# Two-layer hybrid block on one core: the FFN's middle down-projection sums are added to y by DMA after a ScalarE copy, not by VectorE

## The chip, the cores and the metric

The kernel runs on one core of a Trainium2 chip. The metric is the device time of one execution in microseconds (us), taken on the chip; a profile of one execution is kept beside the timed runs. Engines are named as the profile names them: PE is TensorE (matmuls), PEld its weight loads, DVE is VectorE, ACT is ScalarE, POOL is GpSimd and SP is SyncE, which here only issues DMAs. Each engine works through its own list of instructions in a fixed order and waits on semaphores where it needs another engine's result.

## The reference, cut to what matters

Two layers act on x (512 tokens, 1024 channels) and, in the first layer only, on ctx (256 tokens). Each layer has a mixing half (attention, a Fourier mix, a long convolution) and a feed-forward half (the FFN). Only the FFN is touched:

```python
def conv_ffn(h, w_up, w_c, b_c, w_down):
    u = dwconv3(h @ w_up, w_c, b_c)
    gate, val = jnp.split(u, 2, axis=-1)
    return (jax.nn.silu(gate) * val) @ w_down

fx = rmsnorm(x, g_pre_ffn[i]) * (1.0 + sc2) + sh2
yx = conv_ffn(fx, w_up[i], w_ffn_conv[i], b_ffn_conv[i], w_down[i])
x = x + ga2 * rmsnorm(yx, g_post_ffn[i])
```

All numbers are float32, D_FF is 2816, that is 22 blocks of 128 channels. In layer 0 the same is done for ctx.

## The kernel before, in words

**Products.** Float32 products are made of three passes: a matrix is split into a rounded high part and the low rest (`split`, lines 181 and 182: ACT writes the high part, DVE, or POOL where it is given, subtracts to get the low part), and `mm3` (lines 196 to 198) issues high·high, high·low and low·high.

**FFN of x, `ffn_x`.** For each block m of 128 hidden channels, two weight tiles `r` of w_up are loaded by SP, combined by POOL into `tt` (lines 1276 to 1279; the up product is done in a Strassen-like form of seven block products), split by ACT and DVE into `Wh` and `Wl`, and multiplied into four narrow PSUM tiles `pn` (pool of 4 tiles, 128x512) with the activations, which are the streams `h`. ACT and DVE gather the results into `C` (lines 1298 to 1326), ACT and DVE do the depthwise convolution (`ft`, lines 636 to 638), ACT the silu (line 1334), POOL the product of gate and value (line 1335), and ACT and DVE split it into `gT`.

**The down product, `ffn_down`.** It works on groups of blocks: two at a time (in `ffn_x` the last group has four). For a group it loads and splits the rows of w_down (`Wr` to `Wh`, `Wl`), and for each tile t of 128 tokens (4 for x, 2 for ctx) it sums the group's products into a wide PSUM tile `pw` of 128x1024. That pool holds two tiles, so the third t can only begin when the first has been read out. The sums over the groups are gathered in SBUF in `y`, one tile of 128x1024 for each t:

- the first group is copied to `y` by ACT (line 1200),
- each middle group is added to `y` by one DVE instruction (line 1202),
- the last group is added in halves by DVE (line 1196), and goes on to the norm and the residual.

For ctx there are 9 middle groups with 2 tiles, for x 8 with 4 tiles in each of two layers: 18 + 32 + 32 = 82 additions on line 1202.

**FFN of ctx, `ffn_c`,** runs in layer 0 ahead of `ffn_x`, with plain up products (tiles `L` of w_up, product in `pn`, lines 1228 and 1229 for silu and product, `gc` for the split result). There the low parts of w_down are made by POOL. The matmuls that make the modulation (tiles `wm` of w_mod, line 283) run between them.

**Order.** The generators yield estimates of their cost and lag, and `Net.go`, `pump` and `step` interleave them in program order. The tile framework then schedules each engine's list with its own timing model, and adds the waits on semaphores; so the order of the instructions can change when a single one is exchanged. SBUF tiles of 128x1024 come from a pool `M` with 27 buffers, which also holds `y`, `gT`, the streams `h`, the gains `G` and the pieces `w` of w_up. A tile from a pool waits until the last reader of that buffer is done.

Of the kernel before, what the change touches and what calls it, by code (L numbers as in the profile page):

```python
# [8 lines left out]
F32 = mybir.dt.float32  # L9
# [3 lines left out]
ALU = mybir.AluOpType  # L13
# [55 lines left out]
class Net:  # L69
# [1095 lines left out]
    def ffn_down(self, l, st, g, ms, begin, el=None, early=0, mid=None):  # L1165

        nc = self.nc
        end = ms[-1] == MF - 1
        if begin and st is self.X:
            st.y = [self.M("y", F32) for _ in range(st.NT)]  # L1170
        wd = {k: self.load_w(self.I["w_down"][l, k], el=nc.gpsimd if el else None) for k in ms}
        if end:
            ss = [self.small("ss", 2, 6) for _ in range(st.NT)]
            xr = [self.load_r(self.src[st.name][t]) for t in range(st.NT)]
        acc = {}

        def add(t, h, ks):
            hs, ts = slice(h * 512, (h + 1) * 512), slice(t * P, (t + 1) * P)
            if (t, h) not in acc:
                if h == 0:  # L1180
                    acc[t] = self.pw()
                acc[t, h] = acc[t][:, hs]
            for k in ks:
                self.mm3(acc[t, h], (g[k][:, 0, ts], g[k][:, 1, ts]), (wd[k][0][:, hs], wd[k][1][:, hs]), k == ms[0], k == ms[-1])
            yield 3 * len(ks) * C512, 0.0

        for t in range(early):
            for h in range(2):
                yield from add(t, h, ms[:-1])
        for t in range(st.NT):  # L1190
            y = st.y[t]
            for h in range(2):
                hs = slice(h * 512, (h + 1) * 512)
                yield from add(t, h, ms[-1:] if t < early else ms)
                if end:
                    nc.vector.tensor_tensor(y[:, hs], y[:, hs], acc[t, h], op=ALU.add)
                    self.sumsq_half(ss[t], y[:, hs], h)
                    nc.gpsimd.tensor_tensor(y[:, hs], y[:, hs], st.G[1][:, hs], op=ALU.mult)
            if begin:
                nc.scalar.copy(y, acc[t])  # L1200
            elif not end:
                nc.vector.tensor_tensor(y, y, acc[t], op=ALU.add)  # L1202
            else:
                self.tail(st, t, xr[t], ss[t])
                if t == Z["MT"] and mid:
                    yield from mid
# [495 lines left out]
```

## Time and profile before

| | us |
|---|---|
| median of 3 timed runs | 1789.37 |
| lowest and highest of these | 1785.97 and 1790.05 |
| the profiled execution | 1784.91 |
| its span in the trace | 1783.1 |
| its mean granted TensorE clock (share of full) | 0.971 |

Times in the trace are microseconds from the span's start. `ffn_c` fills the stretch from about 480 to 705, `ffn_x` of layer 0 the stretch from there to about 1080, and `ffn_x` of layer 1 that from about 1400 to the end. A group row of the profile names line, engine, operation and tiles, then the count, the busy time and the mean of one, and then how long the engine stood idle just before those instructions and which instruction ended the idle time. A busy PE is not a PE at its peak: the records of matmuls overlap, and the pace of a run of matmuls is read from the distance of their starts.

### The profile page before, as it was taken

Reading aid. Unit: us, or ns where it says so; the run is one execution under the profiler, and the core shown is the slowest. Engines: PE = TensorE matmul, PEld = TensorE weight load, DVE = VectorE, ACT = ScalarE, POOL = GpSimd, SP = SyncE. Lnnn points to the kernel's source line nnn. Section 1 sums busy time; section 2 is a strip of 40 time slices with the busy share of each in tenths; the row PEclk is TensorE's granted clock in tenths of the full one; section 3 lists DMA queues with packets and bytes.
Section 4 is the critical chain, followed back from the end, with each engine's and each line's share of the span. In section 5 each row is a group of like instructions: output and inputs, shape, how many; then the busy total and the mean of one; then the engine's idle time right before and its main releaser. Section 6 shows DMA issues by size and latency. Waiting matters only on the chain. (4 is left out here: it accounts for less than half of the span.)

```text
span 1783.1 us, 27842 instructions
## 1 busy us (share of the span) xinstructions
PE 1639.1 (92%) x10502; PEld 1397.4 (78%) x10502; DVE 1440.1 (81%) x2324; ACT 934.9 (52%) x1737; POOL 692.3 (39%) x515
## 2 busy tenths in 40 slices
PE   5799987899999997989999998998898799999997
PEld 2677775687788897878989885787787678889996
DVE  5888777697665688889988987668895878999997
ACT  2642344487565454556554556434773465555454
POOL 3343332000134337665554645212002455655543
PEclk9899999999999998999999999999999899999999
DMA  9214277603477642332342258653012343332323
GB/s 366 101 61 146 86 243 263 232 13 130 162 253 232 228 155 71 96 118 84 101 148 84 89 185 305 213 175 118 1 48 83 130 146 103 95 107 86 127 62 119
DMA packets 70003, 248.01 MB, mean 139 GB/s; under 512 B 8111, under 2 KB 9647, under 8 KB 69868
## 3 DMA queue, kind: packets, MB, share of 16 engines
q1 hardware_dynamic: 60716, 215.54, 35.6%
q0 software_dynamic: 9152, 30.68, 5.5%
q8 instruction: 83, 1.36, 0.3%
q14 instruction: 52, 0.43, 0.1%
HBM read 232.03 MB, written 14.16 MB: 138 GB/s over the span
## 5 line engine op out<-in xcount | busy, mean ns | idle before, releaser
L196 PE MATMUL pn<-h,Wh 128*128 128x256 f32 x1328 | 376.6, 286 | 11.7 <-DVE ft L638 4.3
L198 PE MATMUL pn<-h,Wl 128*128 128x256 f32 x1328 | 372.8, 284 | 10.2 <-DVE Wl L182 10.2
L197 PE MATMUL pn<-h,Wh 128*128 128x256 f32 x1328 | 374.2, 283 | 1.7 <-POOL h L182 1.7
L196 PEld LDWEIGHTS pn<-h,Wh 128*128 128x128 f32 x1328 | 253.2, 191 | 24.5 <-issue 7.8
L198 PEld LDWEIGHTS pn<-h,Wl 128*128 128x128 f32 x1328 | 252.1, 191 | 15.3 <-DVE Wl L182 12.7
L197 PEld LDWEIGHTS pn<-h,Wh 128*128 128x128 f32 x1328 | 253.8, 191 | 6.2 <-POOL h L182 2.4
L181 ACT CAST Wh<-Wr 128x1024 fp32r<-128x1024 f32 x118 | 122.7, 1049 | 138.9 <-PE pw L198 46.4
L182 DVE TENSOR_TENSOR Wl<-Wr,Wh 128x1024 fp32r<-128x1024 f32 x89 | 129.7, 1465 | 53.7 <-ACT Wh L181 53.2
L1276 POOL TENSOR_TENSOR tt<-r,r 128x512 f32<-128x512 f32 x44 | 75.0, 1705 | 233.9 <-DMA r<-w_up 211.0
L196 PE MATMUL pw<-Wh,gT 128*128 128x512 f32 x352 | 137.5, 404 | 9.0 <-ACT gT L181 3.9
L197 PE MATMUL pw<-Wl,gT 128*128 128x512 f32 x352 | 138.5, 396 | 3.1 <-DVE Wl L182 3.1
L198 PE MATMUL pw<-Wh,gT 128*128 128x512 f32 x352 | 137.8, 396 | 1.8 <-DVE gT L182 1.8
L181 ACT CAST Wh<-tt 128x1024 fp32r<-128x1024 f32 x88 | 90.8, 1048 | 84.9 <-PE pn L197 42.4
L182 DVE TENSOR_TENSOR Wl<-tt,Wh 128x1024 fp32r<-128x1024 f32 x88 | 122.5, 1411 | 11.0 <-ACT Wh L181 8.0
L1335 POOL TENSOR_TENSOR ft<-ft,ft 128x512 f32<-128x512 f32 x44 | 70.8, 1609 | 132.4 <-DVE ft L638 94.2
L1202 DVE TENSOR_TENSOR y<-y,pw 128x1024 f32<-128x1024 f32 x82 | 99.2, 1213 | 20.1 <-PE pw L198 20.0
L182 POOL TENSOR_TENSOR h<-tf,h 128x256 fp32r<-128x256 f32 (+1 forms) x40 | 36.0, 921 | 187.8 <-ACT h L181 186.5
L182 POOL TENSOR_TENSOR Wl<-Wr,Wh 128x1024 fp32r<-128x1024 f32 x29 | 74.6, 2578 | 57.7 <-ACT Wh L181 56.5
L1278 POOL TENSOR_TENSOR tt<-r,tt 128x512 f32<-128x512 f32 x44 | 75.8, 1722 | 51.9 <-DVE Wl L182 51.9
L196 PE MATMUL pw<-h,Wh 128*128 128x256 f32 (+1 forms) x224 | 76.9, 343 | 13.9 <-DVE v L638 2.6
L283 PE MATMUL pn<-wm,cpad 128*32 128x256 f32 x768 | 67.6, 411 | 19.7 <-DMA wm<-w_mod 19.3
L636 ACT ACTIVATE ft<-C,vec 128x512 f32<-128x512 f32 x88 | 68.7, 811 | 32.1 <-DVE C L1325 25.7
(361 smaller groups left out, 4706.1 us busy)
## 6 DMA issues: line engine op xcount, KB each, us to landing
wm<-w_mod SPq DMA_DIRECT2D x96, 512.0 KB, 5.4
r<-w_up SPq DMA_DIRECT2D x90, 512.0 KB, 3.6
Wr<-w_down SPq DMA_DIRECT2D x66, 512.0 KB, 3.8
L<-w_up SPq DMA_DIRECT2D x44, 512.0 KB, 4.4
Wr<-w_out SPq DMA_DIRECT2D x24, 512.0 KB, 3.6
Wr<-w_in_t SPq DMA_DIRECT2D x16, 512.0 KB, 3.9
dft<-hdft_x POOLq DMA_DIRECT2D x16, 512.0 KB, 4.1
Wr<-w_in_c SPq DMA_DIRECT2D x12, 512.0 KB, 3.6
```

The costliest lines, as they stand in the source:

```text
L181: r = nc.scalar.copy(hi, src)
L182: (el or nc.vector).tensor_tensor(lo, src, f32(hi), op=ALU.subtract)
L196: nc.tensor.matmul(ps, l[0], r[0], start=first, stop=False, **kw)
L197: nc.tensor.matmul(ps, l[0], r[1], start=False, stop=False, **kw)
L198: nc.tensor.matmul(ps, l[1], r[0], start=False, stop=last, **kw)
L283: nc.tensor.matmul(ps[32 * g : 32 * g + 32, cs], self.cpad[:, q % 2 * 4 + g, :], w[:, g, :], start=q % 2 == 0, stop=q % 2 == 1, skip_group ...
L636: nc.scalar.activation(dst, ps, AF.Identity, scale=w1, bias=b)
L1202: nc.vector.tensor_tensor(y, y, acc[t], op=ALU.add)
L1276: te.tensor_tensor(half(t13, 0), half(r[1], 0), half(r[0], 0), op=ALU.subtract)
L1278: te.tensor_tensor(half(t24, 0), half(r[1], 1), half(t13, 0), op=ALU.subtract)
L1335: nc.gpsimd.tensor_tensor(o[0], o[0], o[1], op=ALU.mult)
```

## The change

In the middle groups the sum in PSUM is now copied by ACT into a new tile `ya` of pool `M`, and POOL issues a DMA that adds `ya` to `y` in SBUF. The first and the last group are as before. Lines behind it are moved by three: 1276 is 1279 now, 1334 is 1337, 1335 is 1338.

```diff
             if begin:
                 nc.scalar.copy(y, acc[t])
             elif not end:
-                nc.vector.tensor_tensor(y, y, acc[t], op=ALU.add)
+
+                part = self.M("ya", F32)
+                nc.scalar.copy(part, acc[t])
+                nc.gpsimd.dma_start(y, part, accum_op=ALU.add)
             else:
                 self.tail(st, t, xr[t], ss[t])
```

So 82 instructions leave DVE, 82 copies (line 1204) come to ACT, and 82 DMA issues (line 1205) come to POOL. Outside the FFN the order of the instructions is nearly the same as before. What follows shows the fifth middle group of x in layer 1, on three engines.

VectorE before, where the four additions of a group stand between the splits of weights, the convolution and the gathering into `C`:

```order
L182 TENSOR_TENSOR gT_16437<-ft_16429,gT_16437 128x512
L1202 TENSOR_TENSOR y_14734<-y_14734,pw_16454 128x1024
L182 TENSOR_TENSOR w_16626<-r_16609,w_16626 128x512
L1202 TENSOR_TENSOR y_14735<-y_14735,pw_16468 128x1024
L1323 TENSOR_TENSOR C_16539<-C_16539,pn_16554 128x256
L1202 TENSOR_TENSOR y_14736<-y_14736,pw_16482 128x1024
L1325 TENSOR_TENSOR C_16510<-pn_16511,C_16510 128x256
L1326 TENSOR_TENSOR C_16539<-pn_16511,C_16539 128x256
L182 TENSOR_TENSOR Wl_16625<-tt_16617,Wh_16624 128x1024
L637 SCALAR_TENSOR_TENSOR ft_16633<-C_16510,vec_101,ft_16633 128x511
L1202 TENSOR_TENSOR y_14737<-y_14737,pw_16496 128x1024
```

On VectorE the change only takes these four rows out; the others stay in nearly this order. ScalarE at the same place before, from the split of `gT` on (`Wh` are high parts of weights, `ft` the convolution's input, `C` a gathered product):

```order
L181 CAST gT_16437<-ft_16429 128x512
L181 CAST w_16626<-r_16609 128x512
L181 CAST Wh_16624<-tt_16617 128x1024
L636 ACTIVATE ft_16633<-C_16510,vec_101 128x512
L636 ACTIVATE ft_16634<-C_16539,vec_101 128x512
L181 CAST Wh_16622<-tt_16616 128x1024
```

and ScalarE there now:

```order
L181 CAST gT_16569<-ft_16561 128x512
L1204 COPY ya_16599<-pw_16586 128x1024
L1204 COPY ya_16615<-pw_16602 128x1024
L181 CAST Wh_16764<-tt_16757 128x1024
L636 ACTIVATE ft_16773<-C_16650,vec_101 128x512
L636 ACTIVATE ft_16774<-C_16679,vec_101 128x512
L1204 COPY ya_16631<-pw_16618 128x1024
L1337 ACTIVATE ft_16773<-ft_16773 128x512
L181 CAST Wh_16762<-tt_16756 128x1024
L1204 COPY ya_16647<-pw_16634 128x1024
L181 CAST w_16766<-r_16749 128x512
```

Two copies stand together right behind the split of `gT`, which waits for POOL's product of gate and value; the third stands behind the convolution's two first passes, and the fourth three rows later. POOL before, two blocks of the same stretch:

```order
L1335 TENSOR_TENSOR ft_16429<-ft_16429,ft_16430 128x512
L1276 TENSOR_TENSOR tt_16752<-r_16745,r_16744 128x512
L1277 TENSOR_TENSOR tt_16752<-r_16745 128x512
L1278 TENSOR_TENSOR tt_16753<-r_16745,tt_16752 128x512
L1279 TENSOR_TENSOR tt_16753<-tt_16753,r_16744 128x512
L1335 TENSOR_TENSOR ft_16633<-ft_16633,ft_16634 128x512
```

and POOL there now:

```order
L1338 TENSOR_TENSOR ft_16561<-ft_16561,ft_16562 128x512
L1279 TENSOR_TENSOR tt_16892<-r_16885,r_16884 128x512
L1280 TENSOR_TENSOR tt_16892<-r_16885 128x512
L1205 DMA y_14834<-ya_16599 128x1024
L1205 DMA y_14835<-ya_16615 128x1024
L1281 TENSOR_TENSOR tt_16893<-r_16885,tt_16892 128x512
L1282 TENSOR_TENSOR tt_16893<-tt_16893,r_16884 128x512
L1205 DMA y_14836<-ya_16631 128x1024
L1338 TENSOR_TENSOR ft_16773<-ft_16773,ft_16774 128x512
```

On PE, the third sum of such a group began 17 narrow matmuls (128x256) behind the end of the second, and waited for DVE; now it begins 25 narrow matmuls behind it, waits for ACT, and the fourth follows at once. The first sum ends 8 wide matmuls (128x512) ahead of the second in both.

On POOL, the four DMA issues of a group (the fourth follows behind the last row) stand between the four subtractions that make `tt`, and each waits for its copy on ScalarE; the next product of gate and value stands behind three of them.

## The prediction

> **What bounds the kernel now.** I read the page's first part, then a table of the FFN's stretches, then in two of them the matmuls and what ended PE's waits. The page (span; busy time of each engine):
>
> ```profile
> span 1783.1 us, 27842 instructions
> PE 1639.1 (92%) x10502; PEld 1397.4 (78%) x10502; DVE 1440.1 (81%) x2324; ACT 934.9 (52%) x1737; POOL 692.3 (39%) x515
> ```
>
> PE and DVE are both heavily loaded; a share over the whole span doesn't say which holds the FFN. The stretches do (ctx FFN; its end and the start of `ffn_x`; layer 0's first blocks; layer 0's middle groups; layer 1's middle groups):
>
> ```profile
> core 0: us, PE busy (x) PEld busy (x) DVE busy (x) ACT busy (x) POOL busy (x), PEclk, DMA share, GB/s
> 480.00:660.00 180.00, 180.00 (x1324) 158.13 (x1323) 125.87 (x207) 99.69 (x158) 71.78 (x45) 1.00 0.67 226
> 660.00:705.00 45.00, 35.20 (x228) 31.99 (x227) 42.79 (x49) 20.55 (x35) 31.67 (x19) 0.89 0.25 76
> 705.00:790.00 85.00, 77.72 (x536) 72.21 (x536) 67.86 (x73) 49.61 (x80) 54.80 (x32) 0.96 0.32 103
> 790.00:1045.00 255.00, 245.22 (x1653) 223.97 (x1652) 233.41 (x287) 138.82 (x218) 134.29 (x79) 0.99 0.32 104
> 1490.00:1745.00 255.00, 251.49 (x1739) 232.20 (x1738) 237.39 (x261) 135.52 (x212) 128.62 (x77) 1.00 0.30 96
> ```
>
> In the ctx FFN PE never rests and DVE has 30% free. In the two stretches of x's middle groups DVE is busy 92% and 93%, PE 96% and 99%. How much PE could gain is read from its pace, since busy matmuls overlap. A run of narrow matmuls (128x256) and one of wide ones (128x512), first and last starts:
>
> ```profile
> 926.09 0.28 PE L196 MATMUL pn<-h,Wh 128*128 128x256 f32 x1
> ...
> 928.67 0.28 PE L197 MATMUL pn<-h,Wh 128*128 128x256 f32 x1
> ...
> 930.44 0.39 PE L197 MATMUL pw<-Wl,gT 128*128 128x512 f32 x1
> ...
> 935.34 0.39 PE L198 MATMUL pw<-Wh,gT 128*128 128x512 f32 x1
> ```
>
> 22 steps in 2.58 us are 0.117 us for a narrow matmul, 21 steps in 4.90 us are 0.233 us for a wide one. Now the matmuls of layer 0's middle groups, with the idle time before them and what ended it (each of the three passes has its group; those left out have the same count within two):
>
> ```profile
> L196 PE MATMUL pn<-h,Wh 128*128 128x256 f32 x355 | 100.2, 285 | 1.3 <-DVE C L1323 0.6 <-ACT C L1298 0.5 <-ACT C L1316 0.2
> L198 PE MATMUL pn<-h,Wl 128*128 128x256 f32 x354 | 98.4, 284 | 1.4 <-DVE Wl L182 1.4
> L197 PE MATMUL pw<-Wl,gT 128*128 128x512 f32 x126 | 49.7, 399 | 1.1 <-DVE Wl L182 1.1
> L198 PE MATMUL pw<-Wh,gT 128*128 128x512 f32 x126 | 49.4, 396 | 0.9 <-DVE gT L182 0.9
> L196 PE MATMUL pw<-Wh,gT 128*128 128x512 f32 x124 | 48.3, 404 | 5.0 <-ACT gT L181 2.8 <-ACT Wh L181 2.2
> L196 PE MATMUL pn<-h,w 128*128 128x256 f32 x60 | 17.1, 284 | 0.1
> ```
>
> 3x355 + 3x60 = 1245 narrow ones take 146 us at that pace, 376 wide ones 88, and some 32 small ones about 4: 238 of 255 us. So 17 us at most are to be had here; the waits listed are 9.8 of them, 4.0 ended by DVE (0.6+1.4+1.1+0.9) and 5.0 by ACT's `gT` and `Wh`. And layer 1:
>
> ```profile
> L196 PE MATMUL pn<-h,Wh 128*128 128x256 f32 x386 | 106.8, 281 | 1.1 <-DVE C L1323 1.1
> L198 PE MATMUL pw<-Wh,gT 128*128 128x512 f32 x129 | 50.8, 396 | 0.9 <-DVE gT L182 0.9
> L196 PE MATMUL pw<-Wh,gT 128*128 128x512 f32 x130 | 49.9, 399 | 1.5 <-ACT gT L181 0.8 <-DVE y L1202 0.7
> L198 PE MATMUL pn<-h,w 128*128 128x256 f32 x64 | 18.1, 282 | 0.0
> ```
>
> 3x386 + 3x64 = 1350 narrow ones are 158 us, 389 wide ones 91: 249 of 255, so 6 us at most, of which DVE ended 2.7 (1.1+0.9+0.7). **PE bounds the FFN, with DVE close behind it**: what the change can win is PE's few waits, not the DVE time that it frees.
>
> **The change part by part.** What leaves DVE, and what comes to ACT (group of the page; durations min/median/max of the first group's copies):
>
> ```profile
> L1202 DVE TENSOR_TENSOR y<-y,pw 128x1024 f32<-128x1024 f32 x82 | 99.2, 1213 | 20.1 <-PE pw L198 20.0
> ...
> L1200 ACT COPY y<-pw x10: 1002/1008/1017, 508.7 to 1470.7; 128x1024 f32<-128x1024 f32 x10
> ```
>
> DVE loses 82 x 1.213 = 99.2 us. In each of the two stretches that is 32 x 1.213 = 38.8 us: DVE falls from 233 to 195 and from 237 to 199 of 255, 78% at most, and no longer holds PE. ACT gains 82 x 1.008 = 82.7 us, 32.3 in each stretch: 139 to 171 and 136 to 168 of 255. That is hidden in ACT's idle time, as a load; as a place in a queue it isn't, which is the term of new waits below.
>
> Term 1, the hand-over at 700 us, where an addition itself holds PE:
>
> ```profile
> 697.44 4.17 DVE L182 TENSOR_TENSOR w<-r,w 128x512 fp32r<-128x512 f32 x2
> 701.53 2.34 DVE L1202 TENSOR_TENSOR y<-y,pw 128x1024 f32<-128x1024 f32 x2
> ...
> 702.80 0.58 PE L196 MATMUL pw<-h,Wh 128*128 128x256 f32 x1 [2.56 <-DVE y L1202]
> ...
> 705.76 0.37 ACT L1298 COPY C<-pw 128x256 f32<-128x256 f32 x1 [8.27 <-PE pw L198]
> ```
>
> PE waits 2.56 us for a sum to be read while DVE is behind and ACT stands idle for 8.27 us. A copy by ACT removes that wait: -2.6 us. Bounds: 0, and -4.9, since four additions (4 x 1.213) leave a DVE that is 95% busy there.
>
> Term 2, layer 0's middle groups: the 4.0 us ended by DVE go, and of the 5.0 ended by ACT I take half, since `gT` comes late through DVE's convolution but also through POOL: -6.5 us. Bounds: 0 and -17.
>
> Term 3, layer 1's: the 2.7 us ended by DVE go. Bounds: 0 and -6.
>
> Term 4, new waits. Two copies stand behind ACT's split of `gT`, which waits for POOL (total, times, longest, in layer 0's middle groups):
>
> ```profile
> ACT gT L181 <- POOL ft L1335: 35.4, 14, 5.6
> ```
>
> The first sum ends 8 wide matmuls (1.9 us) ahead of the second, and the third starts 25 narrow ones (2.9 us) behind that. So the first copy has 4.8 us, less its own 1.0, before PE notices: a wait of 35.4/14 = 2.5 us is covered, the longest, 5.6, costs PE 1.8 us. Behind the copies on ACT stand the high parts of the next weights, and PE waits for those. I take one such stall: +2 us. Ends: 0, and 1.8 us in all 16 groups of x, +29; a mean that lies inside the cover speaks for the low one.
>
> POOL pays for the issue of each DMA, at the price of its loads (min/median/max in ns):
>
> ```profile
> L716 POOL DMA_DIRECT2D dft<-hdft_x x16: 527/591/956, 79.7 to 1173.0; - x16
> ```
>
> 32 x 0.59 = 18.9 us a stretch, at 0.956 30.6 us, bring POOL from 134 to 153 or 165 of 255; its work on the weights runs a block ahead, which hides it. If that lead is gone, `Wh` is late on ACT; this is inside term 4's ends. Each issue also waits on POOL for its copy, with two subtractions for `tt` and the product for `gT` behind it; the copy is due when the sums end, so this wait replaces POOL's waits for DVE there.
>
> Term 5, the transfers. No accumulating DMA is in this trace. A copy's cost in engine time, from 520 to 660 us (packets, MB, share of the 16 engines), the distance of the ctx groups, and how loads land (count, KB, us) in that stretch and between 790 and 1045 us:
>
> ```profile
> q1 hardware_dynamic: 7918, 28.82, 61.7%
> ...
> L<-w_up SPq DMA_DIRECT2D x29, 512.0 KB, 4.4
> ...
> r<-w_up SPq DMA_DIRECT2D x30, 512.0 KB, 3.6
> ...
> 546.86 1.22 DVE L1202 TENSOR_TENSOR y<-y,pw 128x1024 f32<-128x1024 f32 x1 [0.22 <-PE pw L198]
> ...
> 625.70 1.22 DVE L1202 TENSOR_TENSOR y<-y,pw 128x1024 f32<-128x1024 f32 x1 [0.24 <-PE pw L198]
> ```
>
> 61.7% of 140 us for 28.82 MB is 1.57 us for 512 KB. A ctx group lasts (625.70-546.86)/4 = 19.7 us and leaves 33% of it, 6.5 us, free on the DMA engines: 3.25 us for each of its two accumulations. As one copy (1.57) they fit, as two, since `y` is read as well (3.14), just so; I take that and cost them at nothing. As three (4.7) they exceed it by 2.9 us a group, +26 us over 9 groups. In x's groups (255/8 = 32 us) 68% is free, 5 us for each of four, so there they fit in any case. A `ya` buffer is held from copy to landing; what takes it next stands about ten rows later on ACT (at a copy's 1.0 us, 10 us), more than 4.4 us and the issue.
>
> The Trainium skill, "DMA: Bandwidth & Descriptors", section "Issuing engines are not separate DMA queues", speaks against the change: DMAs of every issuing engine interleave on the same 16 engines, and another issuer saves only issue time. The trace agrees in that loads land in 4.4 us in the ctx FFN (share 0.67) and in 3.6 us at 0.32. That page's section "Anatomy of one DMA" moves bytes at 436 GB/s, 1.2 us for 512 KB as an estimate, 2.4 us for two passes; by that nothing is lost either.
>
> **Sum** on the profiled execution, 1784.9 us (1.8 more than its span): -2.6 - 6.5 - 2.7 + 2 + 0 = -9.8, so 1775.1. The median of the runs shown, 1789.4, lies 4.5 above that execution: **1780 us**.
>
> **Rivals.**
> - **PE's pace is all there is.** The waits that DVE ends come back under another name (`gT` through POOL, `Wh` through ACT), and terms 2 and 3 shrink to nothing: 1789 within 3.6. For it: layer 1 has only 6 us to give. Against it: PE's 2.56 us behind an addition.
> - **All of PE's slack is won:** -4.9 - 17 - 6 = -28, 1761. Against it: 8 of the 17 us are no listed wait.
> - **Slower, by the DMA engines in the ctx FFN.** If an accumulation takes more than 3.25 us of all 16, loads of `L` and `wm` come late and PE, which never waits there now, waits: 1789.4 - 9.8 + 26 = 1806 at three copies' cost. For it: share 0.67. Against it: none of PE's waits there ends with a DMA.
> - **Slower, by ACT's queue:** copies late in half of the 16 groups, at twice 1.8 us, +29, against -11.8: 1806 too.
>
> That the change does not do what it says is ruled out: the lists hold 82 copies and 82 issues, and no addition.
>
> **How the numbers follow.** My forecast (a gain of 4 to 18 us) 0.45, all slack won 0.08, PE's pace alone 0.22, the DMA engines 0.14, ACT's queue 0.11. The two slower cases together are 0.25; faster 0.53; same 0.22, where same means within 0.2%, 3.6 us, about what a measurement of this kernel can tell. The range goes from 1764 to 1803: below it lie most of the case of all slack won, above it the upper half of the slower ones, together some 0.2.
>
> **What would show it.** Right: in 790 to 1045 us DVE near 76%, PE's waits on `Wl` and `gT` mostly gone, the pace of groups in layer 1 unchanged within 1 us, PE without the wait at 700, and PE full in the ctx FFN. Wrong: PE waits whose releaser is the copy or `wm` or `Wh` behind it; landings in the ctx FFN well over 4.4 us; POOL issues well over 0.96 us; a share of the DMA engines near 1 between 480 and 660.

## The result, and the profile after

| | before | after |
|---|---|---|
| median of 4 runs, us | 1788.56 | 1816.20 |
| lowest and highest, us | 1785.97 and 1790.05 | 1810.73 and 1817.48 |
| the profiled execution, us | 1784.91 | 1810.73 |
| mean granted TensorE clock | 0.971 | 0.968 |

The ratio of the runs is 1.015, with a 95% interval of 1.0126 to 1.0174: the changed kernel is 27 us slower. The prediction was 1780 us with a range up to 1803, so it was wrong in sign and range. In what follows, us worked out from a ratio are (ratio - 1) x 1789; a difference of two such values is uncertain by 3 to 6 us.

The page of the changed kernel, span and busy times:

```profile
span 1808.9 us, 28125 instructions
PE 1644.4 (91%) x10502; PEld 1400.6 (77%) x10502; DVE 1382.2 (76%) x2242; ACT 1005.2 (56%) x1821; POOL 732.1 (40%) x597
```

DVE lost 57.9 us, not the 99.2 of its additions; ACT has 70.3 more and POOL 39.8. (Of what DVE did not lose, line 637's 88 convolutions on `C` are 30 us: busy 111.4 us now, 81.3 before; why is open.) The stretches of the prediction, by absolute time (PE, PEld, DVE, ACT, POOL busy, granted clock, DMA share, GB/s):

```profile
480.00:660.00 180.00, 180.00 (x1327) 158.20 (x1326) 113.30 (x195) 112.48 (x172) 81.16 (x59) 1.00 0.87 267
660.00:705.00 45.00, 35.10 (x239) 32.38 (x238) 39.02 (x46) 25.57 (x40) 34.66 (x24) 0.92 0.42 104
705.00:790.00 85.00, 76.41 (x531) 70.09 (x530) 70.64 (x78) 47.94 (x78) 53.57 (x32) 0.98 0.36 113
790.00:1045.00 255.00, 233.49 (x1554) 212.95 (x1553) 203.09 (x239) 157.12 (x237) 138.05 (x102) 0.97 0.60 157
1490.00:1745.00 255.00, 244.89 (x1673) 225.22 (x1672) 206.14 (x215) 149.53 (x229) 147.05 (x108) 0.99 0.62 157
```

In ctx's FFN PE is as full as before, at a DMA share of 0.87. The loss is in x's middle groups. By the starts of x's silus the changed kernel is 3.1 us ahead of before at the first block of layer 0 and 18.2 behind at the last; in layer 1 it goes from 16.3 to 27.2 behind, so layer 0 has two thirds of the loss. In the middle groups' stretches PE is busy 233.5 of 255 us in layer 0 (245.2 before) and 244.9 in layer 1 (251.5 before), though DVE now has a fifth of each stretch free. What ended PE's waits, first in layer 0's stretch, then in layer 1's:

```profile
L196 PE MATMUL pn<-h,Wh 128*128 128x256 f32 x336 | 95.3, 286 | 10.4 <-ACT C L1324 7.7 <-ACT C L1301 1.5 <-ACT Wh L181 1.2
L198 PE MATMUL pn<-h,Wl 128*128 128x256 f32 x336 | 93.4, 285 | 3.7 <-DVE Wl L182 3.6
L196 PE MATMUL pw<-Wh,gT 128*128 128x512 f32 x114 | 45.5, 413 | 5.6 <-ACT ya L1204 5.5
...
L198 PE MATMUL pn<-h,Wl 128*128 128x256 f32 x374 | 103.8, 284 | 7.6 <-DVE Wl L182 7.5
...
L196 PE MATMUL pw<-Wh,gT 128*128 128x512 f32 x120 | 46.7, 400 | 2.5 <-ACT ya L1204 2.5
```

Before, ACT's `gT` and `Wh` and DVE ended these waits. Now in layer 0 it is ACT's gathering into `C` (9.2 us) and the new copies (5.5), in layer 1 the low parts `Wl` (7.5) and the copies (2.5). Which of the change's parts puts them there can't be read from this trace alone, since the scheduler has also put the lists in a new order: with the rows that the change itself adds and removes left out, and by the lines and tile names in the two traces, at least 190 rows of DVE's list and as many of ACT's stand in another order than before.

### The profile page after: what moved, and what is told of

The parts are those of the page before. It is cut to its first block, busy times and chain, and to the rows that moved or that the text cites. A ratio compares the mean times of both kernels' runs of the same rounds, so it can differ in the third digit from the quotient of the medians.

```text
span 1808.9 us, 28125 instructions
## 1 busy us (share of the span) xinstructions
PE 1644.4 (91%) x10502; PEld 1400.6 (77%) x10502; DVE 1382.2 (76%) x2242; ACT 1005.2 (56%) x1821; POOL 732.1 (40%) x597
## 3 DMA queue, kind: packets, MB, share of 16 engines
q1 hardware_dynamic: 60716, 215.54, 34.2%
## 5 line engine op out<-in xcount | busy, mean ns | idle before, releaser
L1279 POOL TENSOR_TENSOR tt<-r,r 128x512 f32<-128x512 f32 x44 | 62.4, 1418 | 260.3 <-DMA r<-w_up 247.1
L196 PE MATMUL pw<-Wh,gT 128*128 128x512 f32 x352 | 140.1, 409 | 15.1 <-ACT ya L1204 9.5
L198 PE MATMUL pw<-Wh,gT 128*128 128x512 f32 x352 | 139.4, 398 | 0.0
L637 DVE SCALAR_TENSOR_TENSOR ft<-C,vec,ft 128x511 f32<-128x511 f32 x88 | 111.4, 1300 | 3.0 <-ACT ft L636 3.0
L1338 POOL TENSOR_TENSOR ft<-ft,ft 128x512 f32<-128x512 f32 x44 | 59.2, 1345 | 128.5 <-ACT ft L1337 56.9
L196 PEld LDWEIGHTS pw<-Wh,gT 128*128 128x128 f32 x352 | 65.5, 190 | 35.2 <-ACT ya L1204 12.6
L182 DVE TENSOR_TENSOR Wl<-L,Wh 128x1024 fp32r<-128x1024 f32 x44 | 60.5, 1376 | 40.5 <-ACT Wh L181 39.7
L1205 POOL DMA_DIRECT2D y<-ya x82 | 72.6, 936 | 44.4 <-ACT ya L1204 41.5
L1204 ACT COPY ya<-pw 128x1024 f32<-128x1024 f32 x82 | 81.1, 1012 | 15.7 <-DMA y<-ya 8.2
L1337 ACT ACTIVATE ft<-ft 128x512 f32<-128x512 f32 x44 | 27.8, 633 | 107.8 <-DVE ft L638 107.8
```

The costliest lines, as they stand in the source:

```text
L182: (el or nc.vector).tensor_tensor(lo, src, f32(hi), op=ALU.subtract)
L196: nc.tensor.matmul(ps, l[0], r[0], start=first, stop=False, **kw)
L198: nc.tensor.matmul(ps, l[1], r[0], start=False, stop=last, **kw)
L637: nc.vector.scalar_tensor_tensor(dst[:, 1:T], ps[:, 0 : T - 1], w0, dst[:, 1:T], op0=ALU.mult, op1=ALU.add)
L1204: nc.scalar.copy(part, acc[t])
L1205: nc.gpsimd.dma_start(y, part, accum_op=ALU.add)
```

## The experiments

### First set: parts of the change, the scheduler free

Theory Q: the copies' places in ACT's list cost the time. Theory P: POOL's issues do. Theory M: the transfers themselves do. Four versions of the three lines:

```diff
 e1_nosum        pass
 e2_copy_only    nc.scalar.copy(part, acc[t])
 e3_issue_small  nc.scalar.copy(part, acc[t]); nc.gpsimd.dma_start(y[:, :8], part[:, :8], accum_op=ALU.add)
 e4_dve_copy     nc.vector.tensor_copy(part, acc[t]); nc.gpsimd.dma_start(y, part, accum_op=ALU.add)
```

> The middle groups' sums are left out: nothing reads the PSUM tile and nothing is added to y. VectorE loses the same 82 additions as with the change, ScalarE, GpSimd and the DMA engines get nothing. This is the most that freeing VectorE can give. If VectorE's additions held PE as the prediction's terms 1 to 3 say, the time is 1789 - 12 = 1777 us, within 1761 (all of PE's listed and unlisted slack) and 1785. If PE's pace is all there is, it is 1789 within 4.

> ScalarE's copies into ya stay, the accumulating DMAs are left out (y lacks the middle groups' sums). Theory Q (the copies' places in ScalarE's in-order list cost it: they stand behind the split of gT and the convolution, and weights and the gathered products stand behind them): most of the 28 us stay, 1805 to 1816 us. Theory P (the issues on GpSimd) and theory M (the transfers themselves): the loss goes, 1775 to 1785 us.

> The copies stay, and each accumulating DMA is issued from the same place, but adds only 8 of 1024 columns (y lacks the other columns' sums): GpSimd's issues stay, the bytes go from 512 KB to 4 KB. Theory M (the transfers): the loss goes, 1775 to 1790 us, and loads of w_up land in 3.6 us again. Theory P (the issues): it stays, 1810 to 1820, while the run with copies alone is near 1780. Theory Q: 1805 to 1816, like the run with copies alone.

> The accumulating DMAs stay as in the change, but VectorE makes the copies into ya, so ScalarE has its work of before. VectorE has 82 instructions more than with the change, as many as before. Theory Q: near before, 1785 to 1795 us. Theories P and M: the loss stays, 1810 to 1825 us, since GpSimd's issues and the transfers are all there.

| run | median, us | ratio to before | interval |
|---|---|---|---|
| e1_nosum | 1799.5 | 1.0059 | 1.0036 to 1.0082 |
| e2_copy_only | 1804.4 | 1.0083 | 1.0058 to 1.0107 |
| e3_issue_small | 1806.6 | 1.0096 | 1.0060 to 1.0133 |
| e4_dve_copy | 1827.3 | 1.0216 | 1.0189 to 1.0242 |

None of the three theories had expected the first row: **with 82 additions left out and nothing put in their place the kernel is 11 us slower than before**. So the order itself had to be a theory (S). The other rows contradict each other: e2 lies just below and e3 inside what theory Q expected, but e4, where DVE copies instead of ACT, is slower still, 32 us above Q's range. Since the scheduler may order each of these kernels anew, their differences don't price a part; from e3 to the change it would be some 10 us for the bytes, and in a fixed order (a2, below) it is 18.

### Second set: the order held as before

The program is now built twice. The first build, with the additions, gives each engine's list; in the second every instruction is tied behind the one that preceded it there, which fixes the order and adds no semaphore. The kernel of before itself was not run in this form. p1 holds all five lists. In p2 to p4 the copies and issues find their own places, and 7% of each list, in layer 0, is left free.

```diff
+    for e, places in order.items():
+        line = [rows[e][p] for p in places]
+        for a, b in zip(line, line[1:]):
+            tc.add_manual_dep(b, a.name, NoSync, reason="order of before")
...
+    _, order = build(False)
+    nc, _ = build(True, order)
```

> The middle groups' sums are left out, as in the first experiment, but every engine's list of instructions stands in the order of before, with the 82 additions taken out. Theory S (the changed kernel's lists were put in a new order, and the new order costs PE time by itself): the time falls from the 1800 of the free order to that of before or under it, 1777 to 1791 us. Theory C (the order is beside the point; what freeing VectorE sets off costs the time): 1797 to 1803 us, as in the free order.

> ScalarE's copies without the DMAs (y lacks the middle groups' sums), the other rows in the order of before, but for some 7% of each list in layer 0, where buffers would run out in it. Theory S with copies that cost little: 1783 to 1793 us, 11 to 20 below the free order. Theory Q (the copies hold ScalarE's queue whatever the order): 1800 to 1806 us, as in the free order.

> Copies, and GpSimd's 82 issues with 8 of 1024 columns each (y lacks the other columns' sums), the other rows in the order of before with the same gap. Theory S: within 4 us of the run before it, since the issues cost little. Theory P (the issues hold GpSimd): 5 to 15 us above the run before it.

> The whole change, with the other rows in the order of before with the same gap. If the new order cost about 13 us and the transfers about 11, this is 1798 to 1806 us. If order is nearly all, it is under 1793; if order is nothing, 1812 to 1820.

| run | median, us | ratio to before | interval |
|---|---|---|---|
| p1_nosum_order | 1774.0 | 0.9908 | 0.9877 to 0.9939 |
| p2_copy_order | 1850.9 | 1.0338 | 1.0314 to 1.0361 |
| p3_small_order | 1856.6 | 1.0371 | 1.0347 to 1.0396 |
| p4_change_order | 1865.4 | 1.0427 | 1.0396 to 1.0457 |

p1 bears theory S out: the same work takes 1774 us in the order of before and 1800 in the order that the scheduler chose without it. p2 missed both of its expectations, the nearer one by 45 us, and p4 all of its. The reason stands in ACT's timeline of a layer 1 group (start, length, idle before it):

```profile
1637.89 1.92 ACT L1207 COPY ya<-pw 128x1024 f32<-128x1024 f32 x2
1642.05 1.02 ACT L1207 COPY ya<-pw 128x1024 f32<-128x1024 f32 x1 [2.24 <-PE pw L200]
1645.68 1.01 ACT L1207 COPY ya<-pw 128x1024 f32<-128x1024 f32 x1 [2.61 <-PE pw L200]
1646.59 0.62 ACT L183 CAST w<-r 128x512 fp32r<-128x512 f32 x1
```

All four copies stand in a row. The third and the fourth wait for PE's sums, and the splits of weights that PE needs next stand behind them. So p2 to p4 don't price the copies but a bad place for them; only their differences count, 6 us for small DMAs (the foot of theory P's 5 to 15) and 10 more for whole ones.

### Third set: copies and issues placed, and the order of the change

For p5 to p7 each copy and each issue gets a place: a copy before the first row of ACT that in the profile of before began later than the addition it replaces, an issue the same way in POOL's list, 1.3 us later. All other rows stand as before, without a gap. `ya` finds no room in pool `M` in that order, so the copies go straight into `y`, and the DMAs add `y` to itself.

```diff
 p5_copy_placed   nc.scalar.copy(y, acc[t])
 p7_small_placed  nc.scalar.copy(y, acc[t]); nc.gpsimd.dma_start(y[:, :8], y[:, :8], accum_op=ALU.add)
 p6_dma_placed    nc.scalar.copy(y, acc[t]); nc.gpsimd.dma_start(y, y, accum_op=ALU.add)
```

> All lists in the order of before, without the gap; in place of the 82 additions ScalarE copies the sums straight into y (so y holds only the last group copied, the sums before are lost), and each copy stands in ScalarE's list where, by the start times of the profile of before, VectorE began the addition. Theory: the copies are cheap where they stand well, and the 1850 us of the copies in the same order came from where they were put: 1774 to 1782 us, near the run without sums. Rival (a copy on ScalarE costs wherever it stands, since it waits there for PE): 1795 us and more.

> All lists in the order of before, the copies and the issues placed as in the two placed runs; each DMA adds 8 of 1024 columns (y lacks the sums). Without issues 1777, with whole DMAs 1790. If the bytes cost the 13 us: 1776 to 1781. If GpSimd's issues do: 1786 to 1791.

> The run before, and behind each copy GpSimd issues an accumulating DMA of 512 KB from y to y (y is doubled), placed in GpSimd's list 1.3 us behind the start of the addition of before. Issues and bytes are those of the change, the order is that of before, and no ya buffer is needed. If the transfers cost 9 to 11 us here too: 1784 to 1793 us. If they cost nothing where the order is good: under 1782. If GpSimd's issues hold its list in this order: above 1800.

The a-runs hold all lists in the order of the changed kernel, and take away one thing at a time. `ya` stays as in the changed kernel, but for a1, which has no such tile, so the step from a1 to a3 holds the copies and the buffers of pool `M` that `ya` takes:

```diff
 a1_nosum  pass
 a3_copy   nc.scalar.copy(part, acc[t])
 a2_small  nc.scalar.copy(part, acc[t]); nc.gpsimd.dma_start(y[:, :8], part[:, :8], accum_op=ALU.add)
 a4_plain  nc.scalar.copy(part, acc[t]); nc.gpsimd.dma_start(y, part)
```

> All lists in the order of the changed kernel, and the 82 copies and the 82 DMAs left out (y lacks the middle groups' sums). If the new order alone costs the time: 1795 to 1805 us, some 25 over the 1774 of the order of before without sums. If order is good and copies and transfers cost the time: 1770 to 1780 us.

> All lists in the order of the changed kernel, the 82 DMAs left out (y lacks the middle groups' sums), the copies in their places. Without copies this order takes 1783 us, with copies and small DMAs 1796. If the copies cost those 12 us: 1793 to 1797. If GpSimd's issues do: 1783 to 1787.

> All lists in the order of the changed kernel, row for row, copies and issues included; each DMA adds 8 of 1024 columns (y lacks the other columns' sums). What is left out is only the bytes. If they cost 9 to 11 us as in the other two pairs: 1804 to 1808 us; if order and copies are all: 1813 to 1818.

> All lists in the order of the changed kernel, row for row; the 82 DMAs carry their 512 KB but copy ya over y and don't accumulate (y holds only the last group copied). Between the small DMAs, 1796 us, and the whole change, 1816. A copy takes 1.57 us of all 16 engines in the profile of before, an accumulation some 2.9 in that of the change. If the engines' time is what costs (loads land later behind it): 1803 to 1809. If 512 KB cost the same either way (the bytes in SBUF, or the waits for the landing): 1812 to 1818.

| what is there | order of before | order of the change |
|---|---|---|
| no sums | p1 0.9908 (-16.5 us) | a1 0.9981, 0.9967 to 0.9996 (-3.4) |
| copies | p5 0.9950, 0.9934 to 0.9966 (-8.9) | a3 1.0017, 1.0003 to 1.0031 (+3.0) |
| copies, small accumulating DMAs | p7 0.9997, 0.9984 to 1.0009 (-0.5) | a2 1.0049, 1.0030 to 1.0068 (+8.8) |
| copies, plain DMAs of 512 KB | - | a4 1.0047, 1.0029 to 1.0065 (+8.4) |
| copies, accumulating DMAs of 512 KB | p6 1.0018, 1.0004 to 1.0032 (+3.2) | the change 1.0150 (+26.8) |

**Leaving the additions out gives 16.5 us. The new order takes back 13.1, the copies 6.4, the issues 5.4 to 5.8 (with plain bytes or hardly any), and the accumulation, over a plain DMA of the same size, 18.4.** Together that is the change's +27. The 16.5 are the most that freeing DVE can give, since nothing reads `pw` in p1 either. Each figure is uncertain by 4 to 6 us, and they are differences along one path: in the order of before copies and issues cost 7.6 and 8.4, much as here, but the accumulations 3.7.

Of the forecasts, a1 (1783.2 us) fell between its two, a2 (1795.9) and a4 (1797.9) below both, and a3 (1792.1) 0.9 below its nearer one. p5 came out as its theory said. p6 (1790.4) met the forecast of transfers at 9 to 11 us, by luck: p7, with next to no bytes, took 1790.2, so that most of it was the issues.

Of the order, one piece is plain in layer 0. ACT in the changed kernel, where the norm of ctx's tail (line 224) meets x's silu (line 1337):

```profile
845.88 1.28 ACT L224 ACT_TABLE_LOAD   x1
847.17 0.29 ACT L224 ACTIVATE rd_y<-ss,rd_x 128x1 f32<-128x1 f32 x1
847.48 1.28 ACT L1337 ACT_TABLE_LOAD   x1
848.78 0.63 ACT L1337 ACTIVATE ft<-ft 128x512 f32<-128x512 f32 x1
849.43 1.28 ACT L224 ACT_TABLE_LOAD   x1
850.72 0.29 ACT L224 ACTIVATE rd_y<-ss,rd_x 128x1 f32<-128x1 f32 x1
850.92 1.03 ACT L181 CAST Wh<-tt 128x1024 fp32r<-128x1024 f32 x1
851.86 0.36 ACT L1324 COPY C<-pn 128x256 f32<-128x256 f32 x1
```

PE's matmul behind that last copy, in the changed kernel and, with the same lists but no sums, in a1:

```profile
852.27 0.58 PE L196 MATMUL pn<-h,Wh 128*128 128x256 f32 x1 [4.67 <-ACT C L1324]
```

```profile
847.69 0.58 PE L197 MATMUL pn<-h,Wh 128*128 128x256 f32 x1 [5.82 <-ACT C L1326]
```

Norm, silu, norm: three loads of a function table at 1.28 us each stand ahead of the copy that frees PE's `pn`. In p1 the two norms stand together, and one load does:

```profile
833.18 1.28 ACT L226 ACT_TABLE_LOAD   x1
834.47 0.48 ACT L226 ACTIVATE rd_y<-ss,rd_x 128x1 f32<-128x1 f32 x2
834.86 1.04 ACT L183 CAST Wh<-tt 128x1024 fp32r<-128x1024 f32 x1
```

There PE has no listed wait between 830 and 870 us. The Trainium skill, "ScalarE: Activation LUTs", section "What ACT_TABLE_LOAD costs", gives about 1283 ns for the load, as the rows do. The changed kernel has 19 such loads, before and p1 have 17, so this piece is 2.6 us of loading and what waits behind it. Most of the order's cost is in layer 0: there, from x's fifth silu to the last, a1 takes 273.0 us and p1 263.7, while in layer 1 a group takes 30.95 us in a1 and 30.99 in p1. The rest of the 13 us stays open.

### Why an accumulation costs more than a copy

The DMA queues and landings between 1510 and 1760 us (packets, MB, share of the 16 engines; count, KB, median us to landing), and POOL's waits for `r` (us, times, longest), in the changed kernel:

```profile
q0 software_dynamic: 4560, 16.65, 37.3%
...
y<-ya POOLq DMA_DIRECT2D x32, 512.0 KB, 5.9
r<-w_up SPq DMA_DIRECT2D x29, 512.0 KB, 5.8
```

```profile
POOL tt L1279 <- DMA r<-w_up: 67.6, 15, 8.5
```

and in a4, in the same order with plain DMAs:

```profile
q0 software_dynamic: 4608, 16.78, 17.5%
...
y<-ya POOLq DMA_DIRECT2D x31, 512.0 KB, 3.2
r<-w_up SPq DMA_DIRECT2D x28, 512.0 KB, 4.1
```

```profile
POOL tt L1283 <- DMA r<-w_up: 49.9, 13, 6.9
```

An accumulation takes 37.3% x 250 / 32 = 2.91 us of all engines, a copy 17.5% x 250 / 32 = 1.37 (16.78 MB are 32 times 512 KB), and the loads of `r` land 1.7 us later. POOL's subtractions wait for them, ACT's `Wh` and DVE's `Wl` for those, and PE for `Wl`. In a group of layer 1, SP issues three of the four loads right behind the fourth accumulation (timeline of POOL and SP):

```profile
1625.04 0.88 POOL L1205 DMA_DIRECT2D y<-ya  x1 [0.77 <-ACT ya L1204]
...
1626.01 3.35 SPq L1272 DMA_DIRECT2D r<-w_up  x3
...
1633.48 1.30 POOL L1279 TENSOR_TENSOR tt<-r,r 128x512 f32<-128x512 f32 x1 [7.57 <-DMA r<-w_up]
```

In a4 POOL's row behind such a burst starts 5.79 us after the burst (1612.42 to 1618.21), here 7.47. So theory L: the fourth accumulation of x's groups is the one that costs. Two runs in the order of the change exchange copies and accumulations:

```diff
 a5_fourth_plain  nc.gpsimd.dma_start(y, part) where st is self.X and t == 3, else with accum_op=ALU.add
 a6_fourth_only   nc.gpsimd.dma_start(y, part, accum_op=ALU.add) where st is self.X and t == 3, else plain
```

> All lists in the order of the changed kernel, row for row; in x's groups the fourth DMA (16 of 82) copies ya over y, the other 66 accumulate (y's last tile lacks sums). Theory L: three loads of w_up are issued 1 us behind each group's fourth accumulation and land late behind it, which holds GpSimd's subtractions and through them PE; the other accumulations meet no load that is waited for. Then most of the 18 us between all copies (1798) and all accumulations (1816) goes: 1798 to 1805 us. Rival (each accumulation costs its share): 1816 less 18 x 16/82 = 1812, 1810 to 1816.

> The reverse: only the fourth DMA of x's groups accumulates (16 of 82), the other 66 copy ya over y (y lacks sums). Theory L: 1810 to 1816 us. Rival (each its share): 1798 + 18 x 16/82 = 1801, 1799 to 1804.

Measured: a5 1808.8 us, ratio 1.0098 (1.0074 to 1.0122); a6 1804.7, ratio 1.0087 (1.0068 to 1.0105). **Neither side's numbers came out**, though both runs lie nearer to those of the rival, that each accumulation costs its share. The 16 fourth accumulations, a fifth of the 82, carry 7 us when they are the only ones and 9 when they alone are missing, so 40 to 50% of the 18.4, where their share would be 3.6; the other 66 carry the rest. Both figures are uncertain by 5 to 6 us. POOL's waits for `r`, in a5 and in a6, grow over a4's 49.9 with the fourth alone by 15.8 of the 17.7 us and without it by 11.2:

```profile
POOL tt L1283 <- DMA r<-w_up: 61.1, 15, 7.3
```

```profile
POOL tt L1283 <- DMA r<-w_up: 65.7, 15, 8.6
```

And the pace of its groups, from the silu of one block to that of the same block six groups on, in the changed kernel:

```profile
1576.65 0.63 ACT L1337 ACTIVATE ft<-ft 128x512 f32<-128x512 f32 x1 [4.15 <-DVE ft L638]
...
1772.03 0.63 ACT L1337 ACTIVATE ft<-ft 128x512 f32<-128x512 f32 x1
```

in a4:

```profile
1564.46 0.63 ACT L1341 ACTIVATE ft<-ft 128x512 f32<-128x512 f32 x1 [2.65 <-DVE ft L639]
...
1752.68 0.63 ACT L1341 ACTIVATE ft<-ft 128x512 f32<-128x512 f32 x1
```

and in a6:

```profile
1577.97 0.63 ACT L1341 ACTIVATE ft<-ft 128x512 f32<-128x512 f32 x1 [3.84 <-DVE ft L639]
...
1771.30 0.63 ACT L1341 ACTIVATE ft<-ft 128x512 f32<-128x512 f32 x1
```

That is 32.56 us a group with all accumulations, 31.37 with none and 32.22 with the fourth alone; a5, without the fourth, takes 31.75 (1580.33 to 1770.80). In layer 1 the fourth accumulation is 0.85 of the 1.19 us a group, and the others 0.38. In layer 0 the shares don't add up: over a4, from x's fifth silu to the last, a6 falls behind by 8 us, a5 by 9 and the changed kernel by 10.5. (Before x's first silu a5 and a6 are already 7 and 4 us behind a4 in these traces, the changed kernel 1; that is not counted here.) One thing that the other accumulations hit there can be seen. ACT's copy waits until an earlier `ya` has landed and its buffer is free, in the changed kernel:

```profile
833.07 1.93 ACT L1204 COPY ya<-pw 128x1024 f32<-128x1024 f32 x2 [3.97 <-DMA y<-ya]
```

a5 has 3.96 us there, a4 and a6 have 2.1, and PE waits 1.14 us behind these copies. Such waits of ACT are 8.2 us in the changed kernel and 4.5 in a4, so they are not the whole; the rest in layer 0 stays open.

p6 tells the collision from the price. In the order of before, between the same times, its accumulations cost the engines 34.2% x 250 / 30 = 2.85 us each and land after 5.9, as in the change, but the loads of `r` land in 3.6 and POOL waits little for them:

```profile
q0 software_dynamic: 4424, 16.09, 34.2%
...
y<-y POOLq DMA_DIRECT2D x30, 512.0 KB, 5.9
r<-w_up SPq DMA_DIRECT2D x27, 512.0 KB, 3.6
```

```profile
POOL tt L1284 <- DMA r<-w_up: 25.4, 12, 4.9
```

Of the loads of `r` issued here 8 of 27 follow an accumulation's issue within 4 us, in the changed kernel 21 of 29. A group of layer 1 takes 31.57 us in p6 and 31.56 in p7, without the bytes: here the accumulations cost nothing. p6 has no `ya`, so by itself it doesn't tell late loads from buffers that come free late; but in layer 1 the changed kernel has no wait for such a buffer.

### The part that held, alone

c1 makes the change in ctx's FFN only (`if st is not self.X`, else the addition by DVE).

> The change in ctx's FFN alone: 18 copies by ScalarE and 18 accumulating DMAs; x's 64 additions stay on VectorE. The scheduler moves some 30 rows of VectorE's list here, not 320. What the hand-over at 700 us gains in the other runs (the blocks of x's first part begin 3 to 4 us earlier than before) stays: 1781 to 1786 us. If the new places of those rows cost as much as they do in the whole change, it is 1789 or more.

Measured: 1788.4 us, ratio 0.9986 (0.9972 to 1.0001), between its two forecasts. It may win 2.5 us, and can't be told from no change. The whole change in the order of before, with its copies well placed, was not tried, since `ya` has no room there; p6, which has its copies, issues and bytes in that order, came out 3 us above before.

## Why the prediction was wrong, step by step

**What bounds the kernel: right.** PE's waits decide, not DVE's load. Without sums and with the lists as before, 99 us less work on DVE gave 16.5 us at most.

**Terms 1 to 3, -11.8: right within the run's uncertainty** (p1: -16.5, interval -22 to -11). By the profile of p1 the gain is 3.9 us up to x's first silu, 4.3 from layer 0's fifth silu to its last and 5.0 in layer 1, against 2.6, 6.5 and 2.7: the sum is better than its parts. At the hand-over PE's wait for `y` at 702.80 is gone in the changed kernel, but a wait at 703.23 stands near it, 1.68 us for DVE's convolution; x's first silu starts at 720.54 instead of 723.65.

**Term 4, +2: mis-sized.** In the order of the change copies and issues cost 12 us (a1 to a2), inside the ends of 0 to +29. The copies do what the rival of ACT's queue said: PE waits for `ya` 5.5 us in layer 0 and 2.5 in layer 1. The 73 us of issues were held to be hidden in POOL's idle time; with 8 columns each, so nearly without bytes, they still cost 6 to 8 us in both orders.

**Term 5, 0: the step that failed.** The price was near: two passes were taken, 3.14 us, and 2.91 were measured. Wrong was to set it against the mean share of the engines that is free, and to put the term at nothing; it measured 18 us. ctx's FFN, where the sum was tightest, showed no loss: PE stayed full at a share of 0.87 (the rival of the DMA engines had the wrong place). x's groups, at a share of 0.6, were said to fit "in any case" and lost 18 us: a transfer that fits on average still delayed the loads it met, and loads of `r` that PE waits for in the end were issued 1 us behind one. At the same price, p6's accumulations cost 3.7 us, in an order where fewer loads follow them. That a `ya` buffer is free again before it is needed failed too, three times in layer 0. The rule of the Trainium skill that was weighed there, in "DMA: Bandwidth & Descriptors", section "Issuing engines are not separate DMA queues", speaks of this interleaving; a4 and the change show it, 4.1 against 5.8 us to landing.

**What the sum left out.** The order was looked at on three engines of one layer 1 group, where little had moved, and no term stood for it: that is the second failed step. It cost 13 us, more than terms 1 to 3 had promised.

**The signs.** Of those named, the wrong ones came: PE waits whose releaser is the copy, and layer 1's groups 1.1 us slower than before (32.56 us against 31.47, 1557.43 to 1746.24), where 1 was the bound. DVE is at 80% in layer 0's stretch, not 76. Loads of `L` in ctx's FFN land in 5.1 us instead of 4.4 and those of `Wr` in 7.2 instead of 4.3, at a share of 0.87, which PE didn't feel. POOL's issues took 0.878 us in the median, half more than the 0.59 they were priced at, and below the bound of 0.956.

## What to carry to other kernels

Where a scheduler sorts the lists, an edit is two changes: its work and a new order. Hold the order of before, or that of after, and take away the parts one by one; here the same work without sums took 1774, 1783 and 1800 us in three orders.

An engine's free time hid a copy here only where it stood behind nothing late and before nothing urgent: with 82 copies and no DMA behind them the kernel took 1777 us where they stood well (p5) and 1851 where they stood badly (p2). The same accumulations cost 18 us where loads that are waited for were issued right behind them and 4 or nothing where fewer were: compare issue times, not mean shares.

## What the runs showed of the hardware that was not expected

An accumulating DMA of 512 KB within SBUF took 2.91 us of all 16 engines and 5.9 us to landing, a plain one 1.37 and 3.2, in the same places. Its issue took POOL longer as well, and not for its bytes. The issues (min/median/max in ns) with accumulation, the changed kernel's:

```profile
L1205 POOL DMA_DIRECT2D y<-ya x82: 853/878/1208, 528.0 to 1756.6; - x82
```

and a4's without:

```profile
L1207 POOL DMA_DIRECT2D y<-ya x82: 527/584/599, 528.8 to 1737.3; - x82
```

An accumulation of 8 columns, in p7, still took 0.873 us to issue.
